# PSUM of a two-layer attention step laid out anew: three two-bank tiles and two single banks instead of two and four

## The chip, the core and the metric

The kernel runs on one core of a Trainium2 chip. The metric is the device time of one execution in microseconds (us). TensorE (PE in the rows, PEld its weight loads) writes its products into PSUM, which has eight banks; VectorE (DVE), ScalarE (ACT) and GpSimd (POOL) compute, SyncE (SP) issues most DMAs. A product is free to be overwritten only when the last engine that reads it is done, so the way in which the banks are shared out sets when TensorE may write next.

## What is computed

640 tokens (512 latent, 128 context) of width 1024 go through two trunk layers. One input projection feeds three head groups; their gated outputs go through one output projection, and a gated residual add ends the layer.

```python
    h = rmsnorm(x, p['norm_g']) * (1.0 + scale) + shift
    parts = jnp.split(h @ p['w_in'], _split_offsets(), axis=-1)
    c_q, c_kv, k_rope, cb, cc, cx, dq, dk, dv, z = parts
...
    o_mla, ckv, kr = mla_branch(c_q, c_kv, k_rope, p['q_norm'], p['w_uq'], p['kv_norm'], p['w_ukv'],
                                rope_mla, ctx_mla)
    o_conv = conv_branch(cb, cc, cx, p['conv_w'])
...
    o_diff, k_d, v_d = diff_branch(dq, dk, dv, p['lam'], p['subln'], lambda_init, rope_diff, ctx_diff)
    mix = jnp.concatenate([o_mla, o_conv, o_diff], axis=-1) * jax.nn.silu(z)
    x = x + gate * (mix @ p['w_out'])
```

The differential heads (`diff_branch`) form two softmax maps per head and take their difference before the values:

```python
        s = jnp.einsum('bqhad,bkhad->bhaqk', qb.astype(jnp.float32), k_f) * scale
        p = jax.nn.softmax(s, axis=-1)
        a = p[:, :, 0] - lam_full * p[:, :, 1]
        return jnp.einsum('bhqk,bkhe->bqhe', a.astype(v_all.dtype), v_all)
```

Latent tokens attend to all latent and to 128 cached context keys; context tokens to context alone.

## The kernel before

**Products.** Each fp32 operand of a projection is split into a high and a low part, and `mm3` (L359 to L364) makes each product from three matmuls. The 640 tokens are done in two halves of 320 columns (`HB`), so one accumulation takes 8 x 3 matmuls of 128x320 and one PSUM bank.

**PSUM.** Two pools: `pps` with two tiles of two banks each (`bank2`), `ppj` with four tiles of one bank (`bank`). A two-bank tile holds the scores `S` of one map (640 columns in two halves) or the five transposes `tp` of a probability tile; single banks hold everything else: projection halves (`p0zd`, `p0qk`, `p0c`, ...), values `v`, attention outputs `O`, the latent-attention queries `qp`, keys `km`, values `vm`, context keys `kc`, the norms' statistics `st` and their broadcast `rb`, and the output projection `wo`.

**Attention.** A unit is one head and one block of 128 queries (u = 0 to 3 latent, u = 4 context). `diff_unit` (L599) writes S0 and S1 of its two maps, takes the maximum (DVE L624, scaled at L625), the exponential E (ACT L631), merges the maps (DVE L636), and at its next turn transposes E on TensorE (L594) and copies the result out (ACT L596); one turn later it multiplies with the values into O (L645), which ACT reads twice (L648, L649). `mla_unit` (L869) does the same with one map, `Sm`, `Em`, `tpm`. The units lie in a list `pipe`: in each step of the loop one new unit issues its scores, projection steps from `main()` follow as a filler, and each unit in `pipe` goes on to its next yield, so O of unit u-2, transposes of u-1 and scores of u stand close together.

**The small products.** `mla_keys` makes, for each pair of heads, two halves `km0`, `km1`, each read four times (twice ACT L850, twice DVE L851). `mla_values` makes six tiles `vm` (ACT L821, then DVE L822). `out_half` (L1149) makes one half of one 128-row block of `wo` and adds it to the residual in DVE L1164 once all its 24 matmuls are done.

**Order.** Instructions are written by these generators and then ordered ahead of the run: an instruction is placed when its tile and its operands are expected to be free, so the number of tiles in a pool changes the order on all engines. On the chip each engine keeps to its list and waits on semaphores. Other DVE work lies between: L153 forms the modulation vectors of the next stage from weights that stream in (`jk<-at,cb`), L142 prepares `cb`, L326 and L274 split weights and the mixed outputs.

Of the kernel before, what the change touches and what calls it, by code (L numbers as in the profile page):

```python
# [20 lines left out]
D = 1024  # L21
# [39 lines left out]
def tile_kernel(ctx: ExitStack, tc: tile.TileContext, i: dict, o: dict):  # L61
# [6 lines left out]
    smp = ctx.enter_context(tc.tile_pool(name="smp", bufs=8))  # L68
    pps = ctx.enter_context(tc.tile_pool(name="pps", bufs=2, space=PSUM))
    ppj = ctx.enter_context(tc.tile_pool(name="ppj", bufs=4, space=PSUM))  # L70
    dr = ctx.enter_context(tc.tile_pool(name="dr", bufs=1, space=bass.MemoryType.DRAM))
# [133 lines left out]

    def rstd_half(accs, n, name):


        pst = bank("st_" + name)
        for c in range(3):  # L210
            for k, acc in enumerate(accs):
                TE.matmul(pst[:, c:c + 1], acc[:, c * 96:c * 96 + 128], ones, start=k == 0, stop=k == len(accs) - 1)
        v = small("v_" + name)
        V.tensor_scalar(out=v[:, 0:3], in0=pst[:, 0:3], scalar1=1.0 / n, scalar2=EPS, op0=ALU.mult, op1=ALU.add)
        y = rsqrt(v[:, 0:3], 3, name)
        yield
        rb = bank("rb_" + name)
        for c in range(3):
            k = 0 if c == 0 else 32
            TE.matmul(rb[:, c * 96 + k:c * 96 + 128], y[:, c:c + 1].to_broadcast([P, P]), ident[:, k:P],  # L220
                      start=True, stop=True)
        return rb[:, 0:HB]

    class Norm:
# [22 lines left out]

        def rstd(self):
            return rstd_half(self.sqs, D, self.name)

# [200 lines left out]

    pas = [bank("pa%d" % cc) for cc in range(4)]
    pts = bank2("pts")
# [29 lines left out]
    now(ab[2])  # L483
    rg = norms[0].rstd()
    next(rg)
# [25 lines left out]
    for l in range(DEPTH):  # L511
# [68 lines left out]
        def qk_head(h):  # L580
# [5 lines left out]
            bg.append(k_post(h, k, res))  # L586

        def transposed(E, nk, name):

            tp = bank2("tp" + name)  # L590
            n = nk // 128
            for c in range(n):
                src = toktile(E, c) if n == 5 else E[:, 0:128]
                TE.transpose(tp[:, c * 128:(c + 1) * 128], src, ident)  # L594
            at = slot("at" + name)
            S.copy(at[:, 0:nk], tp[:, 0:nk])  # L596
            return at

        def diff_unit(h, u, qkh, vt, acc):  # L599
# [38 lines left out]
            yield "T"  # L638
            at = transposed(E[0], nk, "d" + tg)
            yield "O"  # L640
            po = bank("O" + tg)
            n = nk // 128
            for c in range(n):
                vv = vt[c] if u < 4 else vt[5]
                TE.matmul(po[:, 0:128], at[:, c * 128:(c + 1) * 128], vv[:, h * 128:(h + 1) * 128],  # L645
                          start=c == 0, stop=c == n - 1)
            jk = smp.tile([P, P], F32, tag="jk", name="jk" + tg, bufs=2)
            S.activation(jk, po[:, 0:128], AF.Square, accum_out=ss[:, u:u + 1])  # L648
# [220 lines left out]
        def mla_unit(h, u, qq, kk, kc, get_vm, os_, pairs):  # L869
# [25 lines left out]
            if u == 4:  # L895
                at = transposed(e, nk, tg)
            else:
                tp = bank2("tp" + tg)
                for c in range(5):
                    TE.transpose(tp[:, c * 128:(c + 1) * 128], toktile(e, c), ident)  # L900
                if u % 2 == 0:
                    pairs[u // 2] = kh_tile("ph" + tg), qs_tile("pl" + tg, T)
# [5 lines left out]
            if u == 4:  # L908
                po = bank("O" + tg)
                TE.matmul(po[0:64, 0:128], vm[5][:, h * 64:(h + 1) * 64], at[:, 0:128], start=True, stop=True)  # L910
                S.copy(ctxv(os_)[hs_], po[0:64, 0:128])
            elif u % 2 == 1:

                po = bank("O" + tg)
                for c in range(5):
                    for k, t in enumerate(pairs[u // 2]):
                        TE.matmul(po[:, 0:256], vm[c][:, h * 128:(h + 1) * 128].bitcast(F32R),
                                  t[:, :, c * 128:(c + 1) * 128], start=c == 0 and k == 0, stop=c == 4 and k == 1)
                ov = os_[hs_, (u - 1) * 128:(u + 1) * 128]
                S.copy(ov, po[64:128, 0:256])  # L920
# [35 lines left out]
        def main():  # L956
# [4 lines left out]
            for j in range(2):  # L961
                ps = [bank("p%dqk0%d%d" % (l, b, j))[:, 0:HB] for b in range(2)]
                js = slice(j * HB, (j + 1) * HB)
                for kt in range(KT):
# [6 lines left out]
                    if l > 0 and j == 0:  # L971
                        if kt == 2:
                            rg = norms[1].rstd()
                            next(rg)
                        if kt == 6:
                            rbs[1] = now(rg)
                    if l == 0 and j == 0:
# [3 lines left out]
                        if kt == 6:  # L981
                            rg = norms[1].rstd()
                            next(rg)
# [121 lines left out]

        pipe = []
        fins = []
        for g, n, fin in units():
# [4 lines left out]
            adv((n * 2 + 2) // 3)  # L1113
            for p in list(pipe):
                if next(p, "end") == "end":
                    pipe.remove(p)
            pipe.append(g)
# [7 lines left out]
        while pipe:  # L1125
            for p in list(pipe):
                if next(p, "end") == "end":
                    pipe.remove(p)
            adv(3)
# [46 lines left out]
        for _ in sg:  # L1176
            pass
        rg = norms[0].rstd()
        out_half(4, 1, lambda: next(rg))
# [17 lines left out]

    rbs[1] = now(norms[1].rstd())
    for kt in range(KT):
# [116 lines left out]
```

## Time and profile before

| | |
|---|---|
| three runs | 835.64, 831.65, 835.34 us; median 835.34 |
| profiled execution | 832.23 us; its span 830.2 us |
| granted TensorE clock, mean | 0.992 of full speed |
| busy share of the span | PE 94%, PEld 89%, DVE 76%, ACT 54%, POOL 8% |
| DMA | 85.52 MB, mean 103 GB/s |
| chain that ended last | PE 60%, DVE 18%, ACT 9%, DMA 7%, issue 3% |

The span is the time from the first to the last instruction in the trace; 2.0 us lie around it. Waits are listed by the engine that waited and the instruction that ended the wait.

### The profile page before, as it was taken

Reading aid. Unit: us, or ns where it says so; the run is one execution under the profiler, and the core shown is the slowest. Engines: PE = TensorE matmul, PEld = TensorE weight load, DVE = VectorE, ACT = ScalarE, POOL = GpSimd, SP = SyncE. Lnnn points to the kernel's source line nnn. Section 1 sums busy time; section 2 is a strip of 40 time slices with the busy share of each in tenths; the row PEclk is TensorE's granted clock in tenths of the full one; section 3 lists DMA queues with packets and bytes.
Section 4 is the critical chain, followed back from the end, with each engine's and each line's share of the span. In section 5 each row is a group of like instructions: output and inputs, shape, how many; then the busy total and the mean of one; then the engine's idle time right before and its main releaser. Section 6 shows DMA issues by size and latency. Waiting matters only on the chain.

```text
span 830.2 us, 14320 instructions
## 1 busy us (share of the span) xinstructions
PE 783.8 (94%) x5390; PEld 739.3 (89%) x5390; DVE 633.4 (76%) x1494; ACT 445.8 (54%) x978; POOL 70.0 (8%) x45
## 2 busy tenths in 40 slices
PE   6999999989999899999999999999999899999994
PEld 1389988989999888999999998899999899899994
DVE  4788989989998778789567778987778556668535
ACT  2255447454747667674334545546557667756310
POOL 3300011030001102000220002003000200200000
PEclk9999999999999999999999999999999999999997
DMA  8916434132420322135620433411111001111503
GB/s 311 386 66 197 131 104 135 44 92 71 157 83 27 107 90 83 45 120 184 240 102 22 154 103 109 143 30 58 51 59 52 26 26 52 51 53 50 179 1 126
DMA packets 66164, 85.52 MB, mean 103 GB/s; under 512 B 4976, under 2 KB 47408, under 8 KB 66096
## 3 DMA queue, kind: packets, MB, share of 16 engines
q1 hardware_dynamic: 65520, 83.96, 30.9%
q8 instruction: 42, 0.69, 0.3%
q10 hardware_dynamic: 576, 0.66, 0.2%
q14 instruction: 26, 0.21, 0.1%
HBM read 78.14 MB, written 6.46 MB: 102 GB/s over the span
## 4 chain that ended last, share of the span: by engine, by line
PE 60%; DVE 18%; ACT 9%; DMA 7%; issue 3%; POOL 1%; SPq 1%; POOLq 0%; DVEq 0%; ACTq 0%
PE wo L363 5%; PE wo L362 4%; PE wo L364 4%; DVE jk L153 4%; DVE sm L624 2%; ACT E L631 2%; PE O L645 2%; PE p1c L362 2%; PE p1c L364 2%; PE p1c L363 2%; PE tpm L900 2%; PE p1qk L363 2%; PE p1qk L362 2%; PE S L614 2%; PE p1qk L364 2%
## 5 line engine op out<-in xcount | busy, mean ns | idle before, releaser
L153 DVE CUSTOM_DVE_ANT_0 jk<-at,cb 128x512 bf16<-128x512 f32 x128 | 91.9, 718 | 4.9 <-DMA at<-in_adaT 4.2
L631 ACT ACTIVATE E<-S,sm 128x640 f32<-128x640 f32 (+1 forms) x80 | 56.0, 706 | 61.4 <-DVE sm L625 43.3
L363 PE MATMUL wo<-mx,who 128*128 128x320 f32 x256 | 79.3, 311 | 0.1
L364 PE MATMUL wo<-mx,wlo 128*128 128x320 f32 x256 | 79.0, 309 | 0.0
L362 PE MATMUL wo<-mx,who 128*128 128x320 f32 x256 | 78.5, 310 | 0.0
L624 DVE TENSOR_REDUCE sm<-S 128x1 f32<-128x640 f32 (+1 forms) x80 | 55.3, 711 | 3.4 <-PE S L615 2.4
L889 ACT ACTIVATE Em<-Sm,smm 128x640 f32<-128x640 f32 (+1 forms) x40 | 28.3, 708 | 41.9 <-DVE smm L887 40.5
L236 ACT ACTIVATE sqn<-xn 128x320 f32<-128x320 f32 x32 | 15.1, 471 | 64.8 <-DVE xn L1164 64.5
L363 PEld LDWEIGHTS wo<-mx,who 128*128 128x128 f32 x256 | 48.1, 188 | 0.8 <-DVE mx L274 0.6
L614 PE MATMUL S<-kh,qs 128*128 128x320 f32 x128 | 40.7, 327 | 8.5 <-ACT E L631 8.4
L364 PEld LDWEIGHTS wo<-mx,wlo 128*128 128x128 f32 x256 | 48.1, 188 | 0.0
L362 PEld LDWEIGHTS wo<-mx,who 128*128 128x128 f32 x256 | 47.8, 188 | 0.0
L362 PE MATMUL v<-whi_dv,hh 128*128 128x272 f32 x160 | 46.3, 289 | 0.0
L363 PE MATMUL v<-wli_dv,hh 128*128 128x272 f32 x160 | 46.0, 288 | 0.0
L364 PE MATMUL v<-whi_dv,hl 128*128 128x272 f32 x160 | 46.0, 288 | 0.0
L645 PE MATMUL O<-v,atd 128*128 128x128 f32 x336 | 44.1, 275 | 0.2 <-ACT atd L596 0.2
L1164 DVE SCALAR_TENSOR_TENSOR xn<-wo,mod,xn 128x320 f32<-128x320 f32 (+2 forms) x48 | 19.6, 435 | 31.2 <-PE wo L364 21.4
L645 PEld LDWEIGHTS O<-v,atd 128*128 128x128 f32 x336 | 42.1, 192 | 0.5 <-ACT atd L596 0.5
L363 PE MATMUL p0qk<-hl,whi_qk 128*128 128x320 f32 x128 | 40.2, 315 | 2.4 <-DVE hl L394 2.4
L326 POOL TENSOR_TENSOR wli_c<-ri_c,whi_c 128x1024 fp32r<-128x1024 f32 x8 | 19.8, 2475 | 264.7 <-PE p0zm L363 85.4
L362 PE MATMUL p1c<-hh,whi_c 128*128 128x320 f32 x128 | 41.6, 325 | 0.0
L362 PE MATMUL p0c<-hh,whi_c 128*128 128x320 f32 x128 | 41.2, 322 | 0.0
(377 smaller groups left out, 2660.6 us busy)
## 6 DMA issues: line engine op xcount, KB each, us to landing
at<-in_adaT SPq DMA_DIRECT2D x64, 256.0 KB, 4.0
ada<-in_adaA SPq DMA_DIRECT2D x32, 256.0 KB, 5.1
ri_qk<-in_wi SPq DMA_DIRECT2D x16, 512.0 KB, 4.8
ri_c<-in_wi SPq DMA_DIRECT2D x16, 512.0 KB, 4.0
ro<-in_wo SPq DMA_DIRECT2D x16, 512.0 KB, 4.4
ri_dv<-in_wi SPq DMA_DIRECT2D x8, 544.0 KB, 4.6
ri_zd<-in_wi SPq DMA_DIRECT2D x8, 512.0 KB, 3.7
x<-in_xT SPq DMA_DIRECT2D x16, 160.0 KB, 4.8
```

The lines of the kernel that those rows point to most:

```text
L153: V.tensor_tensor_reduce(out=junk, in0=raw, in1=cb2[:, c, :], scale=1.0, scalar=0.0, op0=ALU.mult, op1=ALU.add, accum_out=acc)
L326: eng.tensor_tensor(out=lo, in0=raws[hf], in1=hi.bitcast(F32), op=ALU.subtract)
L362: TE.matmul(ps, ah, bh, start=first, stop=False)
L363: TE.matmul(ps, ah, bl, start=False, stop=False)
L364: TE.matmul(ps, al, bh, start=False, stop=last)
L614: TE.matmul(ps[:, j, 0:HB], qs[:, a, qc], kh[:, a, js], start=True, stop=False)
L624: V.tensor_reduce(out=sm[:, a:a + 1], in_=Sv[a], axis=AX.XY if u < 4 else AX.X, op=ALU.max)
L631: S.activation(ev, Sv[a], AF.Exp, bias=sm[:, 2 + a:3 + a], scale=DIFF_SCALE, accum_out=so)
L645: TE.matmul(po[:, 0:128], at[:, c * 128:(c + 1) * 128], vv[:, h * 128:(h + 1) * 128], start=c == 0, stop=c == n - 1)
L889: S.activation(e if u < 4 else e[:, 0:128], Sv, AF.Exp, bias=sm[:, 1:2], scale=MLA_SCALE, accum_out=sm[:, 2:3])
L900: TE.transpose(tp[:, c * 128:(c + 1) * 128], toktile(e, c), ident)
L1164: V.scalar_tensor_tensor(out=xn[kt][:, a:e], in0=ps[:, a - j * HB:e - j * HB], scalar=mod[l][2][:, kt, c:c + 1], in1=xn[kt][:, a:e], op0=A ...
```

## The change

The pools become three two-bank tiles and two single banks; the total of eight stays. What lived in single banks and has no room there moves to two-bank tiles:

- O of unit u-2 and the transposes of unit u-1 share one tile: transposes in columns 0 to 639, O from column 640 on. The shared tile is taken by the first of the two (`tp_tile`) and given up at the next turn. Columns 512 to 1023 are the second of its banks, so the last transpose and O lie in one bank.
- Since a read may not meet a write in a bank, `stage()` lets all units of `pipe` issue their TensorE work first, up to a new `yield "X"`, and their reads (ACT L596, L648, L649, and DVE's) after that.
- The norms' broadcast `rb` goes to a place handed in as `room`, in two-bank tiles (`pts`, a new `rb0`/`rb1`). The two accumulations of the first projection `qk0` and the start-up tiles `pa` share two-bank tiles.
- Projections, `v`, `qp`, `km`, `vm`, `kc`, `st` and `wo` stay in single banks, of which there are two.

No matmul, transpose, copy or DMA is added or taken away.

```diff
-    pps = ctx.enter_context(tc.tile_pool(name="pps", bufs=2, space=PSUM))
-    ppj = ctx.enter_context(tc.tile_pool(name="ppj", bufs=4, space=PSUM))
+    pps = ctx.enter_context(tc.tile_pool(name="pps", bufs=3, space=PSUM))
+    ppj = ctx.enter_context(tc.tile_pool(name="ppj", bufs=2, space=PSUM))
...
-        rb = bank("rb_" + name)
+        rb = room()
...
-    pas = [bank("pa%d" % cc) for cc in range(4)]
+    pa2 = [bank2("pa%d" % k) for k in range(2)]
+    pas = [pa2[cc // 2][:, cc % 2 * 512:cc % 2 * 512 + 512] for cc in range(4)]
...
+        shared = []
+
+        def tp_tile(name):
+            if not shared:
+                shared.append(bank2("tp" + name))
+            return shared[0]
+
         def transposed(E, nk, name):
 
-            tp = bank2("tp" + name)
+            tp = tp_tile(name)
             n = nk // 128
             for c in range(n):
                 src = toktile(E, c) if n == 5 else E[:, 0:128]
                 TE.transpose(tp[:, c * 128:(c + 1) * 128], src, ident)
+            yield "X"
             at = slot("at" + name)
             S.copy(at[:, 0:nk], tp[:, 0:nk])
             return at
...
-            at = transposed(E[0], nk, "d" + tg)
+            at = yield from transposed(E[0], nk, "d" + tg)
             yield "O"
-            po = bank("O" + tg)
+            po = tp_tile("o" + tg)[:, 640:768]
...
+            yield "X"
             jk = smp.tile([P, P], F32, tag="jk", name="jk" + tg, bufs=2)
             S.activation(jk, po[:, 0:128], AF.Square, accum_out=ss[:, u:u + 1])
...
-                po = bank("O" + tg)
+                po = tp_tile("o" + tg)[:, 640:896]
...
-                ps = [bank("p%dqk0%d%d" % (l, b, j))[:, 0:HB] for b in range(2)]
+                p2 = bank2("p%dqk0%d" % (l, j))
+                ps = [p2[:, b * 512:b * 512 + HB] for b in range(2)]
...
+        def stage():
+
+            shared.clear()
+            read = [p for p in pipe if next(p, "end") == "X"]
+            pipe[:] = [p for p in pipe if p in read]
+            for p in read:
+                if next(p, "end") == "end":
+                    pipe.remove(p)
+
...
-            for p in list(pipe):
-                if next(p, "end") == "end":
-                    pipe.remove(p)
+            stage()
             pipe.append(g)
...
-        rg = norms[0].rstd()
+        rbt = None
+
+        def room():
+            nonlocal rbt
+            rbt = bank2("rb%d" % l)
+            return rbt[:, 0:HB]
+
+        rg = norms[0].rstd(room)
```

The order changes with it. Three places follow. In the changed kernel line numbers are 11 to 22 higher: L624 is L635 there, L625 L636, L835 L847, L847 L859, L594 L604, L645 L656, L1164 L1186.

VectorE in layer 0, around the context unit of head 2 (`sm_2_4`; `shkr`, `kc` belong to the latent attention's rotary keys), before:

```order
L624 TENSOR_REDUCE sm_2_4_1963<-S_2_4_1964 128x1
L153 ISA jk_1905,part<-at_1901,cb_109 128x512
L153 ISA part 128x1
L537 STREAM_SHUFFLE shkr_1945<-kr_1939 32x512
L624 TENSOR_REDUCE sm_2_4_1963<-S_2_4_1964 128x1
L835 COPY kc_2221<-kr_1939 32x512
L625 TENSOR_SCALAR sm_2_4_1963<-sm_2_4_1963 128x2
```

The same place on VectorE in the changed kernel:

```order
L635 TENSOR_REDUCE sm_2_4_1949<-S_2_4_1950 128x1 x2
L153 ISA jk_1889,part<-at_1887,cb_109 128x512
L153 ISA part 128x1
L636 TENSOR_SCALAR sm_2_4_1949<-sm_2_4_1949 128x2
L153 ISA jk_1891,part<-at_1887,cb_109 128x512
L153 ISA part 128x1
L538 STREAM_SHUFFLE shkr_1931<-kr_1925 32x512
L847 COPY kc_2204<-kr_1925 32x512
```

The two maxima and their scaling stand ahead of the shuffle and of the copy `kc`, where they stood between and behind them.

TensorE in layer 0, where the keys `km` of the first pair of heads are made (behind the last `qp` half), before:

```order
L364 MATMUL qp_2928<-cqh_2786,wuql_2755 128x320
L847 MATMUL km_0_2940<-ckA_2043,wuk_831 128x320
L847 MATMUL km_0_2946<-ckA_2043,wuk_831 128x320
L364 MATMUL p0zm_2842<-hh_7_464,wli_zm_2546 128x320
L362 MATMUL p0zm_2971<-hh_0_342,whi_zm_2505 128x320
```

The same place on TensorE in the changed kernel (`tpo` is the shared tile; L656 is O's matmul, L604 the transposes):

```order
L364 MATMUL qp_2905<-cqh_2764,wuql_2734 128x320
L656 MATMUL tpo_3_1_3010<-v_1_500,atd_3_1_2866 128x128
L656 MATMUL tpo_3_1_3010<-v_2_501,atd_3_1_2866 128x128
L656 MATMUL tpo_3_1_3010<-v_3_502,atd_3_1_2866 128x128
L859 MATMUL km_0_2917<-ckA_2028,wuk_825 128x320
L656 MATMUL tpo_3_1_3010<-v_4_503,atd_3_1_2866 128x128
L604 MATMUL tpo_3_1_3010<-idw,E_3_2_2781 128x128 x5
L859 MATMUL km_0_2923<-ckA_2028,wuk_825 128x320
L362 MATMUL p0zm_2948<-hh_0_339,whi_zm_2486 128x320
```

The two `km` halves stood one behind the other in two banks; now six other instructions lie between them, and the second takes the bank of the first.

TensorE at the start of layer 0's output projection, before (`wo_4396`, `wo_4460` and `wo_4495` are its first three accumulations):

```order
L364 MATMUL wo_4460<-mx_4355,wlo_00_4094 128x320
L362 MATMUL wo_4460<-mx_4361,who_00_4093 128x320
L362 MATMUL wo_4495<-mx_4346,who_00_4093 128x320
L363 MATMUL wo_4495<-mx_4346,who_00_4093 128x320
L364 MATMUL wo_4495<-mx_4346,wlo_00_4094 128x320
L363 MATMUL wo_4460<-mx_4361,who_00_4093 128x320
```

The same place on TensorE in the changed kernel (`wo_4359`, `wo_4423` are the first two; the third, `wo_4458`, follows behind the 48th matmul of these):

```order
L362 MATMUL wo_4423<-mx_4324,who_00_4059 128x320
L363 MATMUL wo_4423<-mx_4324,who_00_4059 128x320
L364 MATMUL wo_4423<-mx_4324,wlo_00_4060 128x320
L362 MATMUL wo_4423<-mx_4330,who_00_4059 128x320
L363 MATMUL wo_4359<-mx_4327,who_00_4059 128x320
L364 MATMUL wo_4359<-mx_4327,wlo_00_4060 128x320
```

Three accumulations were interleaved, and now two are; the third starts when both are written. VectorE's list keeps its order there: splits L274, then three `jk` and two `wlo`, then the first L1164.

## Rows read from the trace of the kernel before

**Rows 1.** The page: engines' busy time, and the chain that ended last.

```profile
PE 783.8 (94%) x5390; PEld 739.3 (89%) x5390; DVE 633.4 (76%) x1494; ACT 445.8 (54%) x978; POOL 70.0 (8%) x45
...
PE 60%; DVE 18%; ACT 9%; DMA 7%; issue 3%; POOL 1%; SPq 1%; POOLq 0%; DVEq 0%; ACTq 0%
```

**Rows 2.** TensorE's waits by line: total us, times, longest us.

```profile
PE S L614 <- ACT E L631: 8.4, 6, 3.1
PE tpd L594 <- ACT E L631: 4.7, 4, 2.1
...
PE vm L817 <- DVE vm L822: 3.0, 2, 2.1
...
PE Sm L362 <- DVE smm L887: 1.9, 2, 1.2
...
PE Sm L362 <- ACT Em L889: 0.6, 2, 0.4
```

**Rows 3.** TensorE by stretch: busy us, instructions, clock, DMA share, GB/s.

```profile
386.00:400.00 14.00, 14.00 (x97) 1.00 0.74 246
```

**Rows 4.** Timeline 111 to 136 us (start, us, engine, line; in brackets the wait).

```profile
113.80 0.77 PE L594 MATMUL tpd<-idw,E 128*128 128x128 f32 x5 [1.62 <-ACT E L631]
...
125.80 3.29 DVE L142 TENSOR_TENSOR cb<-cb,tb 128x1024 f32<-128x1024 f32 x1
...
132.19 0.36 ACT L631 ACTIVATE E<-S,sm 128x128 f32<-128x128 f32 x1
...
132.69 0.41 PE L614 MATMUL S<-kh,qs 128*128 128x320 f32 x1 [1.62 <-ACT E L631]
...
133.68 0.34 PE L614 MATMUL S<-kh,qs 128*128 128x320 f32 x1
```

**Rows 5.** Timeline 503 to 523 us: the place in layer 1 that answers to it.

```profile
503.90 0.76 PE L594 MATMUL tpd<-idw,E 128*128 128x128 f32 x5 [2.06 <-ACT E L631]
...
515.71 3.31 DVE L142 TENSOR_TENSOR cb<-cb,tb 128x1024 f32<-128x1024 f32 x1
...
522.62 0.41 PE L614 MATMUL S<-kh,qs 128*128 128x320 f32 x1 [2.00 <-ACT E L631]
```

**Rows 6.** Timeline 171 to 179 us.

```profile
173.44 1.51 DVE L835 COPY kc<-kr 32x512 f32<-32x512 f32 x1
...
174.98 1.11 DVE L625 TENSOR_SCALAR sm<-sm 128x2 f32<-128x2 f32 x1
...
176.99 0.41 PE L614 MATMUL S<-kh,qs 128*128 128x320 f32 x1 [3.11 <-ACT E L631]
```

**Rows 7.** Timeline 74 to 80 us: a value tile begun, an earlier one's copy.

```profile
76.49 0.29 PE L362 MATMUL v<-whi_dv,hh 128*128 128x272 f32 x1
...
78.62 0.39 ACT L711 COPY v<-v 128x272 f32<-128x272 f32 x1
```

**Rows 8.** Timeline 249 to 257 us: the first pair of keys and its readers.

```profile
251.05 1.24 PE L847 MATMUL km<-ckA,wuk 128*128 128x320 f32 x4
...
252.44 0.74 ACT L850 CAST kmh<-km 64x320 fp32r<-64x320 f32 x2
...
253.21 0.72 ACT L854 CAST kmh<-krf 32x640 fp32r<-32x640 f32 x1
...
255.16 0.90 DVE L851 TENSOR_TENSOR kml<-km,kmh 64x320 fp32r<-64x320 f32 x2
```

**Rows 9.** Timeline 269 to 275 us: the readers of the first values.

```profile
271.12 1.11 ACT L821 CAST vm<-vm 128x256 fp32r<-128x256 f32 x3
...
272.69 0.42 DVE L822 TENSOR_TENSOR vm<-vm,vm 128x256 fp32r<-128x256 f32 x1
```

**Rows 10.** Timeline 378 to 390 us: VectorE at the output projection's start.

```profile
379.22 1.70 DVE L274 TENSOR_TENSOR mx<-z0c,mx 128x320 fp32r<-128x320 f32 x4
...
384.93 0.55 DVE L1164 SCALAR_TENSOR_TENSOR xn<-wo,mod,xn 128x320 f32<-128x320 f32 x1
```

**Rows 11.** ScalarE's waits by line: total us, times, longest us.

```profile
ACT jk L648 <- PE O L645: 34.6, 19, 4.3
```

## The prediction on record

> **What bounds the kernel now.** I read the page first. TensorE is busy for 783.8 of 830.2 us, VectorE for 76% and ScalarE for 54%, and the chain that ended last runs through TensorE for 60% and through VectorE for 18% [rows 1]. So TensorE is the bound, but not everywhere. Then I looked at how it works where nothing holds it: over 14 us in the output projection it is busy all the time and issues 97 instructions, one per 0.144 us [rows 3]. The change adds no instruction to TensorE, so only its waits can change. Third, the list of these waits: a score waits for the exponential that still reads a two-bank tile (8.4 us in 6 waits), transposes wait likewise (4.7 us in 4), the latent attention's scores wait 1.9 and 0.6 us, and the values `vm` 3.0 us for VectorE to empty a single bank [rows 2]. The first four sum to 15.6 us, and they are waits on the two-bank pool, which gets a third tile. The last is one on the single banks, which fall from four to two. Last I read the timelines at each long wait, to see whether the tile or the data behind it was late, and the new order for which accumulations now follow one another in one bank.
>
> **What the third two-bank tile gives.** With two tiles, S0 of a unit needs the tile of the previous S1, and the transposes that of S0. With three, each takes a tile that was given up earlier. Not all of 15.6 us comes back:
>
> - At 177 us a score waits 3.11 us. The exponential that it waits for is late because VectorE first copies `kc` (1.51 us) and only then scales the maximum (the row at 174.98) [rows 6]. In the new order the maxima and the scaling stand ahead of the shuffle and the copy. I take 2.8 us, bounds 0 (VectorE is late itself) and 3.1.
> - In front of the two `cb` steps most is lost again. In layer 0 a transpose waits 1.62 us at 113.80 and a score 1.62 us at 132.69; in layer 1 it is 2.06 and 2.00 us [rows 4, 5], together 7.3 us. But VectorE's step L142 of 3.3 us, fed by a DMA, holds up the context unit's exponential until 132.19 + 0.36 = 132.55 us, and the second map's score, which began at 133.68, takes that unit's tile in the new rotation: whatever TensorE won before, it meets this exponential. So 133.68 - 132.55 = 1.1 us is the most; I take 1.0 us here and 1.0 in layer 1, by the same step at 515.71 [rows 4, 5]. Bounds 0 and 7.3 for the two.
> - The other waits of the two lines, 13.1 - 3.1 - 7.3 = 2.7 us: I take half, 1.3, since some of them wait for a maximum rather than a tile. Bounds 0 and 2.7.
> - The latent attention's 1.9 + 0.6 = 2.5 us: all of it, 2.5, since one tile per unit becomes spare. Bounds 0 and 2.5.
>
> Sum of the gains 2.8 + 2.0 + 1.3 + 2.5 = 7.6 us, bounds 0 and 15.6.
>
> **What two single banks cost.** A running projection holds one of the two for some 24 x 0.144 = 3.5 us, so small products must follow one another in the other bank, each only after its readers.
>
> - Keys `km`, first pair of heads, both layers. Now the two halves stand next to each other in two banks, from 251.05 us; the first is written in about half of 1.24 us, at 251.7, and last read at 255.16 + 0.45 = 255.6 [rows 8], 3.9 us later. In the new order the second half waits for the readers of the first. The shortest such chain is two casts of 0.37, the 0.72 cast of the rotary rows between them, and one subtraction of 0.45: 1.9 us [rows 8]. In layer 0 six instructions of about 0.15 lie between (five transposes take 0.77 [rows 4]), 0.9 us. So the wait is from 1.9 - 0.9 = 1.0 to 3.9 - 0.9 = 3.0. I take 2.0, nearer to neither, and 2.0 in layer 1.
> - Keys of the second pair, both layers: 6 projection matmuls, one context score, 5 transposes and 3 score matmuls lie between, about 2.1 us of cover by the same durations. The wait is 0 to 3.9 - 2.1 = 1.8. ScalarE and VectorE serve exponentials in between, so I take the upper half, 1.5 each, 3.0 in all.
> - Values `vm`: six tiles through two banks, one of which is still a projection's at first. A round is the write of about 0.43 us (the first-pair keys' row, a little over half of it for 256 columns: an estimate), the cast of 1.11 / 3 = 0.37 and the subtraction of 0.42 [rows 9], 1.2 us per tile and bank, so two banks give 0.6 us per tile: 3.6 us where writing takes 2.6. Together with the first turn's wait that is 1.2 us beyond today's per layer, 2.4 in all; bounds -3.0 (today's wait goes, since other matmuls now lie between the tiles) and +6.
> - Output projection, layer 0. VectorE splits the mixed outputs until 379.22 + 1.70 = 380.9 us, and its list then goes to the first residual add at 384.93, over at 385.5 [rows 10]. TensorE now fills the time with a third accumulation. With two banks it has done 48 matmuls soon after 380.9, some three of each at the end, at about 381.4, and waits for 385.5: 4.1 us, bounds 0 and 4.1. In layer 1 the list is the shorter; I take 0.8, same bounds.
> - Queries, context keys, statistics, and the values at 76 us. Some eight single tiles follow each other where they had two banks; one reading of 128x320 or less costs 0.37 us by the casts [rows 8, 9], together 2.8 us, bounds 0 and 6. A value tile begun at 76.49 must now wait until ScalarE has copied an earlier one, at 78.62 + 0.39 = 79.0 [rows 7], 2.5 us; this lies ahead of the `cb` step, which takes it up, so it costs nothing, and 2.5 if that cover is gone.
> - O shares a bank with the last transpose, so ScalarE's reads of O start some 0.55 us later (five transposes of 0.77 us less their overlap [rows 4]). ScalarE waited for O 34.6 us in 19 waits, longest 4.3 [rows 11], so it has the time: nothing, and 0.55 for each of some 20 units in one bound, 11 us.
>
> Sum of the losses 4.0 + 3.0 + 2.4 + 4.9 + 2.8 = 17.1 us. Net +9.5. Some of that will be taken up at later points where TensorE waits for VectorE or a DMA in any case (18% and 7% of the chain [rows 1]); I take 1.5 off, a choice, so +8. From the profiled execution's 832.2 that is 840. The runs' median is 835.34, 3.1 above it, with one run at 831.65 on its level; I forecast **841 us**, between 840 and 843.
>
> The Trainium skill, page "Perfetto Trace Analysis", section "Matmuls", asks that independent groups rotate through different PSUM banks, so that one is emptied while the next is written. The `vm` rows agree: four banks were already too few for six tiles. By that rule read strictly every reading of the single banks would lie open, and the sum would be the upper bounds of this part.
>
> **The rivals.**
>
> - *Faster.* The third tile decides: TensorE, always a tile ahead, issues each unit's scores before VectorE and ScalarE ask for them, so that exponentials too start sooner and the later waits go as well. For it: 15.6 us of waits on two-bank tiles in the profile against 3.0 on single banks [rows 2]; 24 x 0.144 = 3.5 us of a projection cover nearly every reading in attention. Against: the `cb` steps, and the key rows. The time: 832.2 less 7.6 to 13, plus 3 to 5 of losses, 822 to 830. It decides if the single-bank losses stay under some 4 us, as when `km` waits only at its shortest chain and VectorE's first add in the output projection is early.
>  The Trainium skill, "Perfetto Trace Analysis", section "Optimization Strategy", says that the same gap coming back on the engine that should be full can mean too little PSUM for the next tile. The ten waits of the first two lines are such a gap, and this rule speaks for this rival.
> - *No change.* Losses and gains meet, or the steps of VectorE pace the stages and TensorE's waits only change their names: 829 to 836.
> - *More than forecast.* The readings take as long as now in all four `km` pairs (12 - 7 = +5), ScalarE comes late to O (+11 at most) and `vm` doubles (+3): 848 to 856.
>
> **How the numbers follow.** Of this kernel 0.5% is 4.2 us, about what a measurement tells from no change. Chances: the forecast (836 to 847) 0.42, more than that 0.10, no change 0.21, faster 0.27. So faster 0.27, same 0.21, slower 0.52. The range for 8 in 10 goes from 825 (gains of 10, losses of 3) to 852; where the forecast's mechanism holds, 836 to 847.
>
> **What would show it.** Right: in the changed trace TensorE's line "S <- ACT E" falls from 8.4 to about 4 us and the wait at 177 is gone; new lines appear, `km` waiting for VectorE some 7 us in four waits and `wo` for VectorE's add 4 us about 381; TensorE's busy time stays near 784. Wrong: no `km` line, or one of the two-bank lines still above 6 us; the third `wo` accumulation starting before 383; ScalarE's exponentials late in every unit. What would make the forecast wrong most easily is the sizing of the readings, since each depends on what ScalarE and VectorE do in that very microsecond in the new order.

## The result, and the profile after

The changed kernel takes 865.52 us (median of four runs, 864.08 to 865.59) against 835.49 for the kernel before. The ratio is 1.0364, 95% interval 1.033 to 1.0398: 30 us slower. The forecast was 841, between 825 and 852; the sign was right, the size a fifth of the loss. The profiled execution took 865.49 us with a span of 863.7. That of the kernel before was a good one (832.23 us at a mean granted clock of 0.992; 18 later runs have 834.35 to 839.58 us at 0.983 to 0.990), so the spans differ by 33.5 us where the medians differ by 30.

The page of the changed kernel, busy time and the granted clock in 40 slices (before: [rows 1]):

```profile
PE 803.8 (93%) x5390; PEld 752.0 (87%) x5390; DVE 632.2 (73%) x1494; ACT 445.1 (52%) x978; POOL 67.8 (8%) x45
...
PEclk9889999999999899999999999999999989999998
```

TensorE runs as many instructions as before and is busy 803.8 - 783.8 = 20.0 us longer. The prediction said that it would stay near 784. The rest of the span, 863.7 - 803.8 = 59.9 us against 46.4, grew by 13.5: those are waits. So of 33.5 us of span, 20.0 are slower work and 13.5 are waiting.

Most of the slower work is in single stretches. TensorE in windows of 2 us of the changed kernel (columns as in [rows 3]):

```profile
44.00:46.00 2.00, 2.00 (x6) 0.50 0.85 246
86.00:88.00 2.00, 2.00 (x11) 0.50 1.05 383
126.00:128.00 2.00, 2.00 (x9) 0.50 0.00 0
290.00:292.00 2.00, 2.00 (x4) 0.50 0.41 133
340.00:342.00 2.00, 2.00 (x9) 0.50 0.68 205
406.00:408.00 2.00, 2.00 (x9) 0.50 0.35 129
692.00:694.00 2.00, 1.99 (x4) 0.50 0.70 248
```

At a clock of 0.50, 1.2 of 2.4 GHz, one 320-column matmul of `wo` starts 0.267 us after another (405.17 to 407.84), and 0.147 us after another at full clock (408.06 to 409.97). With the one at 18.9 us there are eight such stretches inside the work, five of 6.8 us and three of 3.4. TensorE was busy for 40 us of them. The kernel before has one, of 3.4 us, at 524. (Both have one more at the very end, where TensorE has hardly any work.) So of some 36.6 us more at half clock, 45 to 50% was lost: 16.5 to 18.3 us, an estimate, of the 20.0. Where the other 2 to 3 us went was not followed.

What TensorE did ahead of each: its timeline in the changed kernel, the rows with a wait.

```profile
20.31 1.01 PE L212 MATMUL st_n<-ones,sqn 128*128 128x1 f32 x4 [2.85 <-POOL sqn L245]
...
44.00 0.64 PE L362 MATMUL p0qk<-hh,whi_qk 128*128 128x320 f32 x1 [2.54 <-ACT hh L390]
...
83.81 0.63 PE L625 MATMUL S<-kh,qs 128*128 128x320 f32 x1 [2.15 <-ACT kh L577]
...
123.49 0.41 PE L625 MATMUL S<-kh,qs 128*128 128x320 f32 x1 [2.00 <-ACT E L642]
...
287.25 0.70 PE L829 MATMUL vm<-wuv,ckA 128*128 128x256 f32 x2 [2.09 <-DVE vm L834]
...
337.71 0.41 PE L363 MATMUL Sm<-kml,qmh 96*128 96x320 f32 x1 [1.38 <-DVE kml L867]
...
404.74 0.63 PE L362 MATMUL wo<-mx,who 128*128 128x320 f32 x1 [3.78 <-DVE xn L1186]
...
689.78 0.70 PE L829 MATMUL vm<-wuv,ckA 128*128 128x256 f32 x2 [2.08 <-DVE vm L834]
```

Each of the eight stretches begins in one of these waits or some 2 us or less behind its end. Most of the waits are new: for a reader of a late key, value or residual (`kh`, `vm`, `kml`, `xn`), or in the start-up. The last is not: the kernel before has the same wait, at the same place and as long, and kept full clock behind it:

```profile
661.15 1.13 PE L817 MATMUL vm<-wuv,ckA 128*128 128x256 f32 x4 [2.08 <-DVE vm L822]
```

```profile
662.00:664.00 2.00, 2.00 (x14) 1.00 0.64 226
```

The waits by line (before: [rows 2]):

```profile
PE wo L362 <- DVE xn L1186: 7.6, 4, 3.8
PE S L625 <- ACT E L642: 6.3, 6, 2.0
PE vm L829 <- DVE vm L834: 5.0, 4, 2.1
PE km L859 <- issue: 4.6, 2, 2.7
...
PE st_n L212 <- POOL sqn L245: 2.8, 1, 2.8
PE p0qk L362 <- ACT hh L390: 2.5, 1, 2.5
PE S L625 <- ACT kh L577: 2.1, 1, 2.1
```

The line of transposes waiting for E (4.7) is gone and S waits 6.3 instead of 8.4. (For `km` the trace names no releaser, only "issue".) At the place of [rows 6] the score now waits:

```profile
183.91 0.41 PE L625 MATMUL S<-kh,qs 128*128 128x320 f32 x1 [0.33 <-ACT E L642]
```

To see where the time was lost, the start of the same TensorE matmul in both kernels' timelines:

| place | before | changed | later by |
|---|---|---|---|
| first p0qk matmul | 37.67 | 44.00 | 6.3 |
| last v, layer 0 | 88.45 | 99.48 | 11.0 |
| last p0zd | 239.19 | 248.23 | 9.0 |
| first km | 251.05 | 265.63 | 14.6 |
| last vm | 274.35 | 292.73 | 18.4 |
| first wo | 373.74 | 392.64 | 18.9 |
| last wo | 433.26 | 459.60 | 26.3 |
| last p1zd, layer 1 | 629.24 | 653.97 | 24.7 |
| last vm | 662.34 | 695.10 | 32.8 |
| last wo | 817.07 | 850.61 | 33.5 |

The differential heads win (11.0 to 9.0, 26.3 to 24.7); start-up, keys, values and output projection lose. Not all of 9.0 to 14.6 is loss: 13 more TensorE instructions stand ahead of the first `km` than before, some 1.9 us of moved work. From the last p0zd to the last `vm` it is 9.3 us in all, some 5 of them waits.

### The profile page after: what moved, and what is told of

Same layout as the page of the kernel before. It is cut to its first block, busy times and chain, and to the rows that moved or that the text cites. A ratio compares the mean times of both kernels' runs of the same rounds, so it can differ in the third digit from the quotient of the medians.

```text
span 863.7 us, 14332 instructions
## 1 busy us (share of the span) xinstructions
PE 803.8 (93%) x5390; PEld 752.0 (87%) x5390; DVE 632.2 (73%) x1494; ACT 445.1 (52%) x978; POOL 67.8 (8%) x45
## 5 line engine op out<-in xcount | busy, mean ns | idle before, releaser
L153 DVE CUSTOM_DVE_ANT_0 jk<-at,cb 128x512 bf16<-128x512 f32 x128 | 94.9, 742 | 4.1 <-DMA at<-in_adaT 3.3
L635 DVE TENSOR_REDUCE sm<-S 128x1 f32<-128x640 f32 (+1 forms) x80 | 55.6, 710 | 2.5 <-PE S L626 1.4
L625 PE MATMUL S<-kh,qs 128*128 128x320 f32 x128 | 41.5, 333 | 8.7 <-ACT E L642 6.3
L656 PE MATMUL tpo<-v,atd 128*128 128x128 f32 x336 | 44.5, 275 | 1.4 <-DVE mff L690 1.4
L362 PE MATMUL p0qk<-hh,whi_qk 128*128 128x320 f32 x128 | 41.6, 325 | 3.4 <-ACT hh L390 2.5
L656 PEld LDWEIGHTS tpo<-v,atd 128*128 128x128 f32 x336 | 42.3, 191 | 1.8 <-issue 1.6
L1186 DVE SCALAR_TENSOR_TENSOR xn<-wo,mod,xn 128x320 f32<-128x320 f32 (+2 forms) x48 | 19.7, 434 | 30.3 <-PE wo L364 22.6
L326 POOL TENSOR_TENSOR wli_c<-ri_c,whi_c 128x1024 fp32r<-128x1024 f32 x8 | 19.2, 2399 | 287.8 <-PE p0zm L363 91.6
```

The lines of the kernel that those rows point to most:

```text
L153: V.tensor_tensor_reduce(out=junk, in0=raw, in1=cb2[:, c, :], scale=1.0, scalar=0.0, op0=ALU.mult, op1=ALU.add, accum_out=acc)
L326: eng.tensor_tensor(out=lo, in0=raws[hf], in1=hi.bitcast(F32), op=ALU.subtract)
L362: TE.matmul(ps, ah, bh, start=first, stop=False)
L625: TE.matmul(ps[:, j, 0:HB], qs[:, a, qc], kh[:, a, js], start=True, stop=False)
L635: V.tensor_reduce(out=sm[:, a:a + 1], in_=Sv[a], axis=AX.XY if u < 4 else AX.X, op=ALU.max)
L1186: V.scalar_tensor_tensor(out=xn[kt][:, a:e], in0=ps[:, a - j * HB:e - j * HB], scalar=mod[l][2][:, kt, c:c + 1], in1=xn[kt][:, a:e], op0=A ...
```

## The experiments

Theory A: the loss is what the small products wait for in two single banks, and the half clock that stands behind such waits. Rival B: it is the sharing of a tile by O and the next transposes. Rival C: the waits count, and the half clock does not follow from them. Unless it says otherwise, a kernel was run once; the kernel before took 837.0 us beside the first four runs, 839.2 beside the next four, 836.34 (median of 18) beside the three after those and 834.8 beside the last three. Some kernels keep products that nobody reads or tiles held idle; all outputs are computed.

**e4_share_only.** The pools as before, with pa, qk0 and rb in single banks again, and the sharing kept; from the changed kernel:

```diff
-    pps = ctx.enter_context(tc.tile_pool(name="pps", bufs=3, space=PSUM))
-    ppj = ctx.enter_context(tc.tile_pool(name="ppj", bufs=2, space=PSUM))
+    pps = ctx.enter_context(tc.tile_pool(name="pps", bufs=2, space=PSUM))
+    ppj = ctx.enter_context(tc.tile_pool(name="ppj", bufs=4, space=PSUM))
...
-        rb = room()
+        rb = bank("rb_" + name)
```

> The pools go back to two two-bank tiles and four single banks; only the sharing of one tile by O and the next unit's transposes, with TensorE's work of all units ahead of the reads, stays. Theory A (the loss comes from small products that follow one another in two single banks, and from the half clock that their waits bring on): 828 to 840 us, at most one stretch at half clock inside the work, as before the change. Rival B (the loss comes from the sharing: reads of O stand behind the transposes, so VectorE and ScalarE are late in every unit): 850 us or more.

Measured 833.9 us, with two half-clock stretches of 3.4 us (177 and 290 us) where A allowed one. TensorE waits 5.6 us at the shared tile and 3.6 at scores for E, 9.2 against the 13.1 of [rows 2]. The sharing costs nothing: rival B falls. Run twelve times as **e12_share_timed**:

> The kernel of e4 (two two-bank tiles and four single banks as before, O and the next transposes sharing a tile) timed in rounds. In one look it stood 3.1 us below the kernel before, on the same chip. If the sharing helps: ratio 0.993 to 0.998. If that was chance: 0.998 to 1.003.

834.71 us, ratio 0.9994, interval 0.9966 to 1.0021: no gain either.

**e1_wo_room.**

```diff
-            ps = bank("wo%d%d%d" % (l, kt, j))[:, 0:HB]
+            wos.append((kt, j))
+            ps = (bank2 if len(wos) % 3 == 0 else bank)("wo%d%d%d" % (l, kt, j))[:, 0:HB]
```

> The changed kernel, with every third half of the output projection in a two-bank tile. Theory A: the 7.6 us of waits of wo on VectorE's residual add go, and with them the 3.4 us at half clock behind 404 us, which cost 1.7: 865.5 - 9 = 856, between 853 and 859. Rival B: the output projection has no O and no transposes, 863 to 866. Rival C (waits count, the clock does not follow them): 858, and a stretch at half clock stays near 400.

Measured 856.76 us, as A said; rival C's 858 is too near to be told from it by the time, and it is the clock that decides. The waits of wo by line, and TensorE where the changed kernel had the half clock:

```profile
PE wo L362 <- DVE xn L1189: 1.3, 1, 1.3
```

```profile
404.00:406.00 2.00, 2.00 (x16) 1.00 0.54 187
406.00:408.00 2.00, 2.00 (x16) 1.00 0.40 142
```

**e3_vm_room** and **e6_rooms.** `vm` in pairs in two-bank tiles; e6 also has e1's edit and both `km` halves in one tile.

```diff
-                ps = bank("vm%d_%d" % (l, c))[:, 0:256]
+                if c % 2 == 0:
+                    p2 = bank2("vm%d_%d" % (l, c))
+                ps = p2[:, c % 2 * 512:c % 2 * 512 + 256]
```

> The changed kernel, with the six value tiles vm of the latent attention in pairs in two-bank tiles. Theory A: the 5.0 us of waits on VectorE go, and both stretches of 6.8 us at half clock behind 288 and 690 us, each worth 3.4: 865.5 - 11.8 = 854, between 850 and 858. Rival C: 865.5 - 5.0 = 860.5, with half-clock stretches still within 20 us of these places. Rival B: 863 to 866.

> The changed kernel with three of its small products in two-bank tiles: the two halves of each km in one, vm in pairs, every third half of wo. Theory A: waits of wo 7.6, vm 5.0 and km with its readers some 8, and four half-clock stretches worth 10 us go: 865.5 - 30 = 836, between 831 and 845. Rival C: 845 and no fewer half-clock stretches. Rival B: 860 or more.

Measured 860.52 and 854.66 us, both misses for A. The first is rival C's number, but neither run tests A or C, since the waits had not gone: `vm` still waited 4.1 and 4.2 us for VectorE, and in e6 `km` 4.3, because the second matmul of a tile waited for the reads of the first, though in another bank. That is a matter of how the edit wrote them, and says nothing of the chip.

**e7_rooms2.** The matmuls of a tile are written ahead of its reads, for `km` and `vm`; e1's edit; and e5's start-up.

```diff
+            p2 = bank2("km" + tg)
+            for j in range(2):
+                TE.matmul(p2[:, j * 512:j * 512 + HB], wuk[:, ws], ckA[:, j * HB:(j + 1) * HB], start=True, stop=True)
             for j in range(2):
                 js = slice(j * HB, (j + 1) * HB)
-                ps = bank("km%d" % j + tg)
+                ps = p2[:, j * 512:j * 512 + 512]
```

> The changed kernel with the start-up of the run before this one, every third wo half in a two-bank tile, and km and vm in pairs in two-bank tiles with both matmuls of a tile written ahead of its reads (in the earlier runs the second matmul of a tile waited for the reads of the first, though in another bank). Theory A: start-up 6, wo 9, vm 12 and km 8 us come back: 865.5 - 35 = 831, between 826 and 840. Rival C (waits count, the clock does not follow them): 842 to 850.

847.85 us: 17.7 of the 30 come back, less than A said, and the total lies in rival C's range; the start-up's loss was still there. But the clock did follow: of 17.6 us less span 9.4 are TensorE's busy time (794.4 us against 803.8, with the same 5390 instructions) and 8.3 are waits, and five half-clock stretches are left of eight.

**e5_start** and **e10_start2.** The broadcast in a single bank, and pa paired anew (e5) or the last pa in a single bank (e10, shown).

```diff
-    rg = norms[0].rstd(lambda: pts[:, 512:512 + HB])
+    rg = norms[0].rstd(lambda: bank("rb_s")[:, 0:HB])
...
-    pas = [pa2[cc // 2][:, cc % 2 * 512:cc % 2 * 512 + 512] for cc in range(4)]
+    pas = [pa2[0][:, 0:512], pa2[1][:, 512:1024], pa2[1][:, 0:512], bank("pa3")]
```

> The changed kernel with another start-up: the norm's broadcast rb in a single bank rather than in the tile pts of the modulation's transposes, and the four pa in other pairs, so that two that are in work at the same time lie in different tiles. Theory D (the shared tiles of the start-up hold the first projection back by 6.3 us, and bring on two stretches of 6.8 us at half clock): first p0qk matmul at 37 to 39 us instead of 44.0, total 865.5 - 6 = 859.5, between 856 and 862; the half clock at 83 us stays, since the score ahead of it still waits for kh. Rival E (the cb step at 125 us, which a DMA feeds, takes the delay up): 864 to 866.

> The changed kernel with the start-up's last pa in a single bank and the norm's broadcast in the other, so that TensorE's order there is again two pa matmuls ahead of the norm's statistics st_n. Theory F (the order at 17 us, which left TensorE idle for 2.85 us ahead of st_n and brought on the half clock, is the start-up's loss): first p0qk matmul at 37 to 40 us instead of 44.0, no half clock at 19 us, and the last v matmul at 93 to 96 instead of 99.5; total 859 to 863. Rival E (the first cb step takes it up): total 864 to 867 although p0qk starts earlier.

e5: 866.74 us, first p0qk at 43.4; st_n still stood ahead of the pa matmuls, and waited 3.9. Theory D as put (the tile of the transposes) falls. e10 has the old order there, and the first projection is in time:

```profile
36.69 0.42 PE L362 MATMUL p0qk<-hh,whi_qk 128*128 128x320 f32 x1
```

No half clock at 19 us. So the order at 17 us was the start-up's loss. Yet the total is 865.01, outside theory F's range and inside rival E's: the lead of 7.3 us at the first projection is 4.0 at the first v, 3.8 at the last, 3.2 at the last p0zd, 2.1 at layer 0's last vm and 0.8 at layer 1's first p1qk. Rival E's reason does not fit: much of the lead is lost by the first v, at 49 us, ahead of every cb step. The other waits are still there, new half-clock stretches came at 421 and 547 us, and that behind wo's wait lasts 6.8 us, not 3.4. What one place gives, the places behind it can take away.

**e8_fill_vm** and **e9_fill_wo.** Matmuls with no reader where TensorE waits, for the question of the clock (e8: 14 behind the first `vm`; e9: 26 behind the second half of wo).

> The changed kernel with 14 more 320-column matmuls, whose product nobody reads, between the first and the second value tile vm in each layer, where TensorE waits 2.1 us: 14 x 0.144 = 2.0 us of work in place of the wait. Theory A (the half clock is brought on by TensorE's wait): the stretches of 6.8 us at half clock behind 288 and 690 us go, worth 3.4 each, and the kernel with more work is faster: 859, between 856 and 862. Rival C (the clock falls for another reason): 865 to 868, and both stretches stay.

> The changed kernel with 26 more 320-column matmuls, whose product nobody reads, behind the second half of layer 0's output projection, where TensorE waits 3.8 us for VectorE's residual add: 26 x 0.144 = 3.7 us of work, about as long as the wait. Theory A: the stretch of 3.4 us at half clock behind 404 us goes, total 865.5 - 1.7 = 863.8, between 862.5 and 865. Rival C: 865 to 868, and the stretch stays.

e8: 879.98 us, outside both ranges, because the filler was not the one meant: each of its matmuls runs as two, as those of `km` and `vm` do, and it takes 7.7 us in each layer instead of 2.0.

```profile
283.11 7.70 PE L831 MATMUL fill<-ckA,wuv 128*128 128x320 f32 x28
```

In layer 0 the second vm moved ahead of other work, and a wait of 4.0, with a half-clock stretch behind it, took the place of 2.1. In layer 1 the wait of 2.1 is down to 0.3 and no half clock stands behind it. e9: 866.34, above A's range and in rival C's, though not with C's clock. Its filler covers the wait (0.64 left of 3.78) and the half clock behind 404 us is gone; but the next wait of wo, 2.23 us at 420.65, now has one. A half answer.

**e13_hold_wo** and **e14_hold_wo_fill.** So the same in the kernel before: two of its four single banks are held through layer 0's first halves of wo. e14 adds e9's filler.

```diff
+        held = [bank("hold%d" % k) for k in range(2)] if l == 0 else []
+        for h in held:
+            TE.matmul(h[:, 0:2], ident, ident[:, 0:2], start=True, stop=True)
...
+            if kt == 1:
+                for k, h in enumerate(held):
+                    TE.matmul(h[:, 0:2], ident, xn[1][:, 0:2], start=True, stop=True)
+                    S.copy(small("held%d" % k)[:, 0:2], h[:, 0:2])
```

> The kernel before, with two of its four single banks held (written at the start of layer 0's output projection, and read only when the residual of its second row block is done), so that the first halves of wo go through two banks; nothing else is changed. Theory A: the wait that the changed kernel shows at 404 us appears here, 3.5 to 4.1 us ahead of the third half, with a stretch of at least 3.4 us at half clock behind it: the stage is 5 to 8 us longer. Rival C (the wait alone): 3.5 to 4.1 us longer, no half clock within 5 us of it.

> The same with 26 matmuls of 320 columns, whose product nobody reads, behind the second half of wo, 23 of which stand in TensorE's list where it waits. The third half can start no earlier, so that only the state of the clock differs. Theory A: no half clock behind the place, and the stage 1.7 to 3.4 us shorter than in the run without the filler, though it holds 3.7 us more work. Rival C: as long as without, or longer, and the half clock stays if it was there.

Timeline and windows of e13:

```profile
391.15 0.64 PE L362 MATMUL wo<-mx,who 128*128 128x320 f32 x1 [3.77 <-DVE xn L1164]
```

```profile
392.00:394.00 2.00, 2.00 (x10) 0.50 0.13 47
394.00:396.00 2.00, 2.00 (x9) 0.50 0.90 277
```

The same of e14:

```profile
382.61 3.53 PE L1181 MATMUL fillw<-mx,who 128*128 128x320 f32 x23
...
386.44 0.41 PE L362 MATMUL wo<-mx,who 128*128 128x320 f32 x1 [0.30 <-DVE xn L1164]
```

```profile
388.00:390.00 2.00, 2.00 (x16) 1.00 0.49 164
390.00:392.00 2.00, 2.00 (x16) 1.00 0.54 164
```

From the first to the last wo matmul of the layer it is 59.5 us before, 64.9 with two banks held (379.68 to 444.53), and 62.8 with two banks held and the filler (374.97 to 437.73). The third half begins 11.5 us behind the first in both. With 3.7 us more work TensorE is 2.1 us sooner done, since it stays at full clock: 5.4 us longer than before without the filler and 2.1 shorter with it, both as A said. Theory A holds at this place, and rival C falls. The totals, 846.44 and 836.78, differ by more than this: e13 has further half-clock stretches at 178 (6.8 us), 277, 516 and 673, e14 at 40, 177 and 511, at places that the filler does not touch.

**e15_hold_kv.** The kernel before, two single banks held from the first `km` to the last `vm` of layer 0.

> The kernel before, with two single banks held from layer 0's first keys km to its last value vm; nothing else is changed. Theory A: TensorE waits some 2 us for km and some 2 us for vm as in the changed kernel, and at least one half-clock stretch lies between 250 and 300 us: the way from the first km to the last vm, 23.3 us before, takes 27 to 33. Rival G (the changed order of the scores, not the banks, makes these waits): 23 to 25 us, and no half clock there.

844.65 us. Its timeline:

```profile
258.89 0.78 PE L857 MATMUL km<-ckA,wuk 128*128 128x320 f32 x2 [1.73 <-issue]
...
280.41 0.70 PE L817 MATMUL vm<-wuv,ckA 128*128 128x256 f32 x2 [1.44 <-DVE vm L822]
```

From the first km to the last vm it is 29.4 us (255.74 to 285.15) against 23.3 before. Of these 6.1 us 3.3 are waits (5.1 against 1.8), and some 2 are 14 more instructions that the order now puts between the two places. Without those it is 27.4, still above rival G's 25: two held banks make such waits without the shared tiles, and rival G falls. But there is no half clock there at all, which A had asked for.

**e11_all_rooms.** The changed kernel with e7's rooms, e10's start-up, and every third `v` in a two-bank tile.

```diff
-                ps = bank("v%d%d%d" % (l, b, c))[:, 0:272]
+                ps = (bank2 if (b * 5 + c) % 3 == 2 else bank)("v%d%d%d" % (l, b, c))[:, 0:272]
```

> All rooms together on the changed layout: the start-up of the run before this one, wo's every third half and every third value accumulation v in a two-bank tile, km and vm in pairs in two-bank tiles with matmuls ahead of reads. TensorE's list then has the first score behind the last v again. Theory A (all of the loss is single banks and the half clock behind their waits): 832 to 840, at most two half-clock stretches inside the work, ratio 0.995 to 1.005 to the kernel before. If something else of the change costs (the sharing, the third tile's order): 845 or more.

841.66 us (median of five runs), ratio 1.0053, interval 1.0035 to 1.0071, just outside what A said in time, and with four half-clock stretches where A allowed two. Of the 30 us 24 are back, with the sharing and the third two-bank tile still in place, so most of the loss is not theirs. The 4 to 5 us that are left are clear of noise, and no run shows what costs them. With the first score again behind the last v, the last v is at 89.4 us (99.5 changed, 88.5 before). The stretches last 3.4 us each; new waits of 4.6 us (p0c, for VectorE) and 3.0 (O, for ScalarE) came in. No version was shown to beat the kernel before; e12 is level with it.

## Why the prediction was wrong

**The step that failed** is "The change adds no instruction to TensorE, so only its waits can change". The prediction took each wait at its own length, with TensorE's busy time "near 784", and put the price of a wait to the work behind it at nothing. Measured: 803.8 us with the same 5390 instructions. It read the granted clock of [rows 3] as 1.00 and did not look what a wait does to the work behind it. The trace of before held the sign: behind the wait of 2.00 us at 522.62 [rows 5] its clock stood at 0.50:

```profile
524.00:526.00 2.00, 2.00 (x10) 0.50 0.03 8
```

This term is 20.0 of 33.5 us, 16.5 to 18.3 of them by the estimate above at half clock; without it the forecast's range would have held (865.5 - 20.0 = 845.5). That a wait brings the half clock on is shown at one place, the third half of wo: e13 and e14, and e1, where wait and stretch go together. For the other seven stretches it is argued from where they lie. e10, where the stretch at 19 us goes with st_n's wait, and layer 1 of e8 support it.

**The waits** were forecast at a net 8 and came to 13.5 (59.9 - 46.4). One sum is wrong: the gains 2.8 + 2.0 + 1.3 + 2.5 are 8.6, not 7.6, so by the prediction's own terms the net was +7 and the forecast 840; this does not change where the result lies. The gains were sized well; the losses were too small.

- The score at 177 us: 3.11 to 0.33, as forecast (2.8).
- The `cb` places: 1.62 and 1.62 us became 2.00 (123.49) and 0.95 (141.94) in layer 0, 2.06 and 2.00 became 1.50 and 1.18 in layer 1: a gain of 1.7, forecast 2.0. The wait at 141.94 is for the context unit's exponential, as the prediction had it; the one at 123.49 is for a latent unit's. The 3.3 us of step L142 were misread (last section). The lines S and tpd together fell by 6.8 us; forecast 6.1 for the first three items. The table shows less of it (2.0 and 1.6), in layer 0 after a half-clock stretch at 126 that cost some 1.6. The prediction named "one of the two-bank lines still above 6 us" as a sign of being wrong, and S is at 6.3.
- The latent attention: the waits of 1.9 and 0.6 are gone, as forecast (2.5), but two for `plm`, 0.90 and 1.00, stand where one of 0.5 did.
- First pair of `km`: 4.6 us in two waits, 1.91 and 2.67; forecast 2.0 each. Second pair: it is the scores that wait, 1.38 and 0.51 us in layer 0 and 0.51 in layer 1, for the readings `kml` and `kmh` of the late half; forecast 1.5 each. e15 shows two banks as the cause for the first pair in layer 0.
- `vm`: 5.0 us against 3.0; forecast +2.4. The sum was right in size, but not the reason: the 2.08 in layer 1 stood before, with four banks, and both waits of 2.1 end behind a step of VectorE that took 2.2 us (last section). With vm in pairs of banks (e7, e11) vm no longer waits, but the scores wait 1.2 to 2.0 us for its late reading. In the changed kernel each of the two waits carries 6.8 us at half clock.
- wo in layer 0: 3.78 us at the place forecast, 4.1; e13 and e1 show the two banks as the cause. A second wait of 2.54 at 423.07 was not forecast. Layer 1: 0.89 and 0.40, forecast 0.8.
- Queries, context keys and the other single tiles: `qp` 0.74, ckq's 0.57 and 0.88, p1zd 1.08 and two under 0.2, together 3.6; forecast 2.8.
- The start-up was not priced: its order changed too, st_n went ahead of two pa matmuls, and the first projection started 6.3 us late. The order is fixed before the run, and the prediction had not looked there. e10 shows that this order was the cause.
- "A value tile ... costs nothing": the wait for ScalarE's copy is 0.5 us, but a score had been drawn into the gap, and waited 2.15 us for `kh` at 83.81, and half clock came with it. The `cb` step did not take this up: of 11.0 us at the last v, 9.0 are there at the last p0zd.
- O behind the transposes: nothing, as forecast (e4).

Of the rivals, "more than forecast" had the right side and the wrong mechanism: none of the three readings that it doubled did.

**What stays open.** Why a wait brings on the half clock at one time and not at another. At 177 us the kernel before waited 3.11 us and kept full clock; e13 waited 3.10 at the same place and fell to 0.50:

```profile
178.00:180.00 2.00, 2.00 (x11) 0.50 0.00 0
```

The 2.08 us for vm in layer 1 brought it on in the changed kernel and not in the kernel before. And in the changed kernel waits of 2.54 (wo, 423.07) and 2.67 (`km`, 671.77) kept full clock where 2.00 and 1.38 did not.

In the five other kernels of this study that kept wo's wait of 3.77 to 3.80 (the changed one, e3, e5, e8 and e10), each run or profiled once, a half-clock stretch stands at it every time, and none in the six in which this wait is gone or short (e1, e6, e7 and e11 with room, e9 and e14 with filler); e15's `km` and `vm` waits of 1.4 to 1.7 had none. The sum over a kernel can thus not be worked out from waits alone, and single runs of kernels that differ by 5 us are hard to rank.

## What to carry to other kernels

On a kernel whose TensorE is full, a wait can have two prices: its own length, and the work behind it at half clock; so read the granted clock behind each wait, before the sum of the waits. Before banks are taken from small products, look at how long their readers hold them, not only at what waits most now: 8.4 + 4.7 us of waits at the two-bank tiles fell to 6.3, and were traded for more at products that are small but are read by two engines in turn. When an order is worked out ahead of the run, every stage is to be looked through, also those which the change does not mean.

## What the runs showed of the chip that was not expected

A half-clock stretch lasted 3.4 to 10.2 us (e5, at 20 us; e15, at 176), so what it costs, up to half its length, can be more than the wait ahead of it: some 3 us, for 6.8 us behind a wait of 2.09. A filler of 3.5 us of useless matmuls at a wait made a stage 2.1 us shorter.

And small steps of VectorE stood still beside GpSimd. The wait for `vm` at 287.25 follows an instruction on 128x5 elements that took 2.21 us, where its like take 0.17. It ended at 286.46, as GpSimd's long subtraction ended at 286.44.

```profile
284.25 2.21 DVE L197 TENSOR_TENSOR w_d<-y_d 128x5 f32<-128x5 f32 x1
...
286.50 0.17 DVE L198 TENSOR_TENSOR w_d<-w_d,e 128x5 f32<-128x5 f32 x1
```

```profile
281.58 4.86 POOL L326 TENSOR_TENSOR wli_c<-ri_c,whi_c 128x1024 fp32r<-128x1024 f32 x2 [91.59 <-PE p0zm L363]
```

The same stands ahead of the wait at 661.15 in the kernel before:

```profile
655.52 4.82 POOL L326 TENSOR_TENSOR wli_c<-ri_c,whi_c 128x1024 fp32r<-128x1024 f32 x2 [83.37 <-PE p1zm L363]
```

```profile
658.17 2.20 DVE L197 TENSOR_TENSOR w_d<-y_d 128x5 f32<-128x5 f32 x1
```

In the sixteen profiles of this study, 50 steps of VectorE on 128x5 elements take more than 0.4 us. Each of them overlaps an L326 of GpSimd and ends 0.02 to 0.03 us behind it, though not every such step beside one is held. The long `cb` step that the prediction priced [rows 4] has one beside it too: L142 took 3.29 us beside the L326 that began ahead of it, and 1.22 us in the changed kernel, where GpSimd began only at 135.37:

```profile
125.20 2.80 POOL L326 TENSOR_TENSOR wli_qk<-ri_qk,whi_qk 128x1024 fp32r<-128x1024 f32 x1 [15.32 <-ACT whi_qk L324]
```

```profile
135.12 1.22 DVE L142 TENSOR_TENSOR cb<-cb,tb 128x1024 f32<-128x1024 f32 x1
```

That GpSimd holds VectorE up is argued from these ends; no run moved L326 to test it.
